# SiLU gates evicted by ACT alone, and the first attention queries prepared ahead of a branch

## The chip, the cores and the metric

The kernel runs on one core of a Trainium2 chip. The metric is the device time of one execution in microseconds (us). The engines are named as in the profile: PE (TensorE; its weight loads are PEld), DVE (VectorE), ACT (ScalarE), POOL (GpSimd) and SP (SyncE, which here only issues transfers). Each engine works through its own queue in order, and so does SP's queue of transfers.

## The reference, cut to what matters

One layer with 1024 prompt tokens and 64 sample tokens, width 1024, all in float32:

```
mod = silu(c) @ w_mod + b_mod                    # shift, scale, gate
h = rms_norm(x) * (1 + scale) + shift
z = h @ w_in     # q, k, v, indexer, zga, u, zgs, zma, zmb
o = sparse attention: 256 keys a query, chosen by a top-k of indexer scores
branch_a = (o * silu(zga)) @ w_attn_proj
y = state-space scan over u                      # complex diagonal, 64 states a group
branch_b = (glu(gelu(y)) * silu(zgs)) @ w_ssm_proj
x + gate * ((sigmoid(zma) * branch_a + sigmoid(zmb) * branch_b) @ w_out)
```

The change touches how `silu(zga)` and `silu(zgs)` are formed, when `gate` is computed, and when the first queries are rotated. What is computed stays the same.

## The kernel before

**Products as filler.** Every float32 product is made of three products of rounded halves (`mm3_parts`, L199): high by high, high by low (L202, L203) and low by high (L207). The projections of `h` that nothing waits for soon (q, u, zma, zmb, zga, zgs) are a list of 32 jobs of 128 columns, worked by one generator, `late` (L209, L634 to L645). A job has three chunks of 384, 384 and 320 tokens; a chunk is 24 matmuls in three **steps** of 8, and `next(late)` emits one step. The list has 288 steps. After a chunk its `evac` empties the PSUM tile `acc`, of which there are two (L100). The weights of the next job are loaded by SP into `raw` (L163, two buffers), rounded by ACT into `whi` (L157), and POOL makes the rest, `wlo` (L158). The jobs run in this order: q (4), u (4), 14 of zma and zmb, zga (4, `gate_a`), zgs (4, `gate_s`), and the last two of zma and zmb.

**The two gates.** `gate_a` (L616) and `gate_s` (L625) take the sigmoid of `acc` on ACT, then DVE multiplies it by `acc` (L621, L630); only then is `acc` free. `gate_a` goes on to POOL, which multiplies the attention output `oT` (L622); `gate_s` stores to DRAM.

**The stages after the keys.** First come the indexer scores, then the k and v projections. The top-k (L887) is a long run of DVE passes that ends in a branch on a value that DVE computes (`arms`, L967, with `select` inside). `N_TOPK` steps of filler are emitted ahead of the top-k beyond the q jobs, and `N_BR` steps after the branch: 6, and 6 + 9 + 4. Between those, `gates` (L1157) computes the gate row in two halves: a 2 MB load `gw`, 8 matmuls (L1172), a copy, a matmul by `sel` (L1177), a bias that DVE adds (L1180), a store. After the branch the pool `atq` is opened (L1204), in space that the top-k's tiles held. In it `att_queries` (L1002) loads a block of queries and its rotation table (L1006 to L1011), POOL rotates them (L1012 to L1014), and ACT and DVE split them (`stack_queries`, L254 to L260). `build_keys` (L986) transposes and splits the keys. Then `attention` runs, woven with filler.

**After attention** comes the state-space branch: `ssm_scan` (L1387), a serial chain on DVE, `ssm_fix` (L1406) for four groups q, and `ssm_out` (L1426), in which SP moves `zs` to `zq` (L1432) and PE multiplies (L1440, L1441). Filler is woven in at 3.2 steps a piece (L1469). Then the GELU (L1488: ACT, then two DVE passes that make `ghi` and `glo`), woven with filler at 3 steps, the rest of the filler (L1497), and the GLU products, which read `ghi` and `glo`. There POOL also makes `olo` (L1541), whose space is free when the last filler matmul has read `h`.

**What sets the order.** The program is traced in the order of the code, and a scheduler then fixes every engine's queue before the run: it goes by that order, but moves an instruction ahead where, by its own durations, an engine would be idle. So the queues hold an order that was planned with other durations than the chip's.

Of the kernel before, what the change touches and what calls it, by code (L numbers as in the profile page):

```python
# [33 lines left out]
P = 128  # L34
# [15 lines left out]
N_PRE = 6  # L50
N_TOPK = 6
N_BR = (6, 9, 4)
R_ATT = 1.15
# [30 lines left out]
def hybrid_step(ctx, tc, ins, outs):  # L84
# [27 lines left out]
    def bank1():  # L112
        return tpb().rearrange("p a b -> p (a b)")
# [23 lines left out]
    shcol = small.tile([P, KD, 2], F32, name="shcol")  # L137
    scs = small.tile([P, KD, 32], F32, name="scs")
    pool.memset(scs, 0.0)
    nhalf = small.tile([P, 1], F32, name="nhalf")  # L140
# [305 lines left out]
    c4 = small.tile([P, KD, 4], F32R, name="c4")  # L446
    dve.tensor_copy(c4[:, :, 0:2], scs[:, :, 0:2])
    c_rest = dve.tensor_tensor(c4[:, :, 2:4], scs[:, :, 0:2], c4[:, :, 0:2].bitcast(F32), op=OP.subtract)

# [17 lines left out]
    pool.memset(cz, 0.0)  # L467
    dve.tensor_copy(cz[:, :, 0:2], scs[:, :, 0:2])
    scr = rb.tile([P, 6, 512], F32, tag="t1", name="scr")
# [146 lines left out]
    def gate_a(m):  # L616

        def evac(c, t0, n, ps):
            s = tmp("sg")
            act.activation(s[:, :n], ps[:, :n], AF.Sigmoid)  # L620
            dve.tensor_tensor(s[:, :n], ps[:, :n], s[:, :n], op=OP.mult)  # L621
            pool.tensor_tensor(oT[:, m, t0:t0 + n], s[:, :n], oT[:, m, t0:t0 + n], op=OP.mult)  # L622
        return w_in, C_GA + m * P, evac

    def gate_s(m):  # L625

        def evac(c, t0, n, ps):
            s = tmp("sg")
            act.activation(s[:, :n], ps[:, :n], AF.Sigmoid)
            dve.tensor_tensor(s[:, :n], ps[:, :n], s[:, :n], op=OP.mult)  # L630
            sync.dma_start(gs_d[m, :, t0:t0 + n], s[:, :n])
        return w_in, C_GS + m * P, evac
# [36 lines left out]
    vnew = kvp.tile([64, 2, 64], F32, name="vnew")  # L669

    tk_ctx, ix_ctx = ExitStack(), ExitStack()
    tkp = tk_ctx.enter_context(tc.tile_pool(name="tkp", bufs=1, side="right"))
# [329 lines left out]
    def att_queries(b):  # L1002
# [10 lines left out]
        pool.tensor_tensor(qt[:, :, :nq], qt[:, :, :nq], cs, op=OP.mult)  # L1013
        pool.tensor_tensor(qt[:, :, :nq], qt[:, :, :nq], qw[:, :, :nq], op=OP.add)  # L1014
        st = atq.tile([P, 4, 2, P], F32R, tag="qs", name="qs")
        stack_queries(st, qt, 4, 4, nq)
        mx = small.tile([P, 4, 8], F32, tag="mx", name="mx", bufs=2)
        return st, mx

# [137 lines left out]
    def gates():  # L1157


        sel = small.tile([P, 2], F32, name="sel")  # L1160
        for b in range(2):
            dve.tensor_reduce(sel[:, b:b + 1], ident.rearrange("p (g r) -> p g r", r=32)[:, :, b],
                              axis=mybir.AxisListType.X, op=OP.add)
        for h in range(2):
            cols = slice(2 * D + h * 512, 2 * D + h * 512 + 512)
            ps = bank1()
            w = tokp.tile([P, KD, 512], F32, tag="wtok", name="gw")
            sync.dma_start(w, w_mod[:, cols].rearrange("(k p) c -> p k c", p=P))
            yield
            for k in range(KD):  # L1170
                g = 32 * (k % 4)
                pe.matmul(ps[g:g + 32], scs[:, k, :], w[:, k], start=(k < 4), stop=(k >= 4), skip_group_check=True)  # L1172
            yield
            r = wpool.tile([P, 528], F32, tag="raw", name="grow", bufs=RAW)[:, :512]
            act.copy(r, ps)
            o = bank1()[0:2]
            pe.matmul(o, sel, r, start=True, stop=True)  # L1177
            bm = wpool.tile([P, 528], F32, tag="raw", name="gbias", bufs=RAW)[0:2, :512]
            sync.dma_start(bm, ins["b_mod"][:, cols].to_broadcast([2, 512]))
            dve.tensor_tensor(bm, o, bm, op=OP.add)  # L1180
            sync.dma_start(gate_d[:, h * 512:h * 512 + 512], bm)
            yield

# [7 lines left out]
    kvs = kv()  # L1191
    run(kvs)
    while done[0] < n_q:
        next(late)
    q_stored = stored[0]
    for _ in range(N_TOPK):
        next(late)
    tk = topk(ixp)
    gate_steps = gates()
    next(gate_steps)  # L1200
    run(tk)
    ix_ctx.close()
    tk_ctx.close()
    atq = at_ctx.enter_context(tc.tile_pool(name="atq", bufs=2, side="right"))  # L1204
    for n, half in zip(N_BR, (3, 2, 0)):
        for _ in range(n):
            next(late)
        for _ in range(half):
            next(gate_steps, None)

    qw = wpool.tile([P, 4, P], F32, tag="ub", name="qw", bufs=1)
    pool.memset(qw, 0.0)
    kst = rb.tile([P, 2, 2, 1024], F32R, tag="t2", name="kst")
    build_keys(kst, None, [(ktok[:, t], P) for t in range(8)])
    with tc.issue_after(q_stored.ins):
        ready = att_queries(BO[0])

# [4 lines left out]
    def heads():  # L1222
# [4 lines left out]
        for i, b in enumerate(BO):  # L1227
# [6 lines left out]
            for h in range(8):  # L1234
                other = Head(b, h, st, mx, keys, vals, pt, other)
                yield other
                if h == QH and b < 8:
                    ready = att_queries(BO[i + 1])
                if h == VH and b == 8:
# [454 lines left out]
```

## Time and profile before

| | us |
|---|---|
| median of 3 runs | 1081.34 (1080.79 to 1082.34) |
| the profiled execution | 1083.0 |
| its span | 1081.2 |
| PE, PEld, DVE, ACT, POOL busy in the span | 987.0, 891.0, 673.0, 457.5, 290.6 |
| mean granted TensorE clock | 0.958 of full speed |

The span goes from the first to the last instruction; 1.8 us of the profiled execution lie outside of it. A busy engine is one with an instruction in it; for PE this includes time at half clock, so a stretch in which PE is busy throughout can still lose time. Where PE is idle, the view of waits names the engine and line whose end came last ahead of the waiting instruction.

### The profile page before, as it was taken

To read this page: it belongs to the slowest core of one execution; us is meant where nothing else is said; L and a number is where in the kernel's file an instruction comes from. 1 tells how busy PE (TensorE), PEld (TensorE's weight loads), DVE (VectorE), ACT (ScalarE), POOL (GpSimd) and SP (SyncE) were. 2 spreads that over 40 slices of the span, in tenths; PEclk is the share of its full clock that TensorE was granted. 3 is DMA by queue.
4 is the path that set the end of the run, shared out by engine and by line. 5 is a ranking of instruction groups with operands and counts; after the bars stand their busy time and mean duration, and the time that the engine had idled before them with its cause. 6 is when DMAs were issued, how large, how long until landed. Compare 5 with 4: busy or idle time off the path is not lost.

```text
span 1081.2 us, 16676 instructions
## 1 busy us (share of the span) xinstructions
PE 987.0 (91%) x5948; PEld 891.0 (82%) x5948; DVE 673.0 (62%) x1426; ACT 457.5 (42%) x973; POOL 290.6 (27%) x433
## 2 busy tenths in 40 slices
PE   7777999998799999999999991799997999999997
PEld 1466887998579999999898991799996999998786
DVE  6764888899247778877647799610107566654243
ACT  3575667221147666666533220122244344442122
POOL 3474202622330211222116260564114000001200
PEclk9797999998899999999999996899998999999999
DMA  8731201142451211112147331144764245534133
GB/s 294 220 92 30 77 2 47 52 160 63 133 125 26 62 54 51 56 59 80 57 99 125 97 97 25 43 96 97 166 188 118 88 148 168 160 105 156 53 128 112
DMA packets 141766, 108.41 MB, mean 100 GB/s; under 512 B 32894, under 2 KB 128680, under 8 KB 141680
## 3 DMA queue, kind: packets, MB, share of 16 engines
q1 hardware_dynamic: 140160, 105.05, 34.6%
q10 hardware_dynamic: 1232, 2.23, 0.6%
q8 instruction: 47, 0.77, 0.3%
q14 instruction: 39, 0.32, 0.1%
q0 software_dynamic: 288, 0.05, 0.0%
HBM read 77.79 MB, written 25.17 MB: 95 GB/s over the span
## 4 chain that ended last, share of the span: by engine, by line
PE 62%; DVE 22%; ACT 4%; issue 4%; POOL 3%; DMA 2%; SPq 2%; DVEq 0%; POOLq 0%; ACTq 0%
PE acc L202 12%; PE acc L207 12%; PE acc L203 11%; PE o L1084 4%; PE big L207 3%; PE big L203 3%; PE big L202 3%; PE tp L1067 3%; PE sc L1041 3%; DVE gt L910 2%; DVE near_v L917 2%; DVE sc L708 1%; PE big L695 1%; DVE t L1379 1%; DVE below L919 1%
## 5 line engine op out<-in xcount | busy, mean ns | idle before, releaser
L202 PE MATMUL acc<-hhi,whi 128*128 128x384 f32 (+1 forms) x768 | 258.8, 341 | 41.7 <-DVE sg L621 29.4
L203 PE MATMUL acc<-hlo,whi 128*128 128x384 f32 (+1 forms) x768 | 252.6, 333 | 0.0
L202 PEld LDWEIGHTS acc<-hhi,whi 128*128 128x128 f32 x768 | 147.0, 191 | 49.8 <-DVE sg L621 30.1
L207 PE MATMUL acc<-hhi,wlo 128*128 128x384 f32 (+1 forms) x768 | 148.2, 332 | 0.9 <-POOL wlo L158 0.9
L203 PEld LDWEIGHTS acc<-hlo,whi 128*128 128x128 f32 x768 | 147.1, 192 | 0.5
L158 POOL TENSOR_TENSOR wlo<-raw,whi 128x512 fp32r<-128x512 f32 x64 | 87.9, 1389 | 193.9 <-ACT whi L157 104.9
L207 PEld LDWEIGHTS acc<-hhi,wlo 128*128 128x128 f32 x768 | 128.5, 188 | 2.2 <-POOL wlo L158 1.5
L157 ACT CAST whi<-raw 128x512 fp32r<-128x512 f32 x64 | 38.2, 619 | 87.1 <-PE acc L203 49.3
L1071 ACT CAST pt<-tp 128x512 fp32r<-128x512 f32 (+3 forms) x112 | 49.4, 453 | 41.7 <-PE tp L1067 40.5
L1072 DVE TENSOR_TENSOR pt<-tp,pt 128x512 fp32r<-128x512 f32 (+3 forms) x112 | 57.1, 519 | 14.0 <-ACT pt L1071 12.7
L1051 ACT ACTIVATE pm<-pm,mx 128x1024 f32<-128x1024 f32 (+8 forms) x72 | 56.2, 780 | 20.0 <-DVE mx L1044 19.7
L1629 POOL TENSOR_TENSOR yh<-yh,gfin 128x512 f32<-128x512 f32 (+1 forms) x9 | 11.6, 1293 | 183.2 <-ACT xr L1625 183.2
L612 ACT COPY st<-acc 128x384 f32<-128x384 f32 (+1 forms) x60 | 27.7, 462 | 77.0 <-PE acc L207 72.7
L1044 DVE CUSTOM_DVE_ANT_0 pm<-sc,bias 128x512 f32<-128x512 f32 (+4 forms) x72 | 42.7, 594 | 26.0 <-PE sc L1041 24.9
L203 PE MATMUL acc<-wolo,mhi 128*128 128x512 f32 (+2 forms) x152 | 58.0, 386 | 0.0
L202 PE MATMUL acc<-wohi,mhi 128*128 128x512 f32 (+2 forms) x152 | 57.4, 381 | 0.0
L1041 PE MATMUL sc<-kst,qs 128*128 128x512 f32 (+3 forms) x192 | 52.1, 351 | 2.0 <-DVE mx L1044 1.3
L1067 PE MATMUL tp<-ident,pm 128*128 128x128 f32 (+2 forms) x328 | 53.0, 269 | 0.8 <-DVE pt L1072 0.6
L1084 PE MATMUL o<-pt,vst 128*128 128x256 f32 x288 | 47.6, 291 | 1.4 <-DVE pt L1072 1.2
L1067 PEld LDWEIGHTS tp<-ident,pm 128*128 128x128 f32 (+2 forms) x328 | 38.9, 139 | 9.5 <-DVE pt L1072 2.1
L708 DVE SCALAR_TENSOR_TENSOR sc<-relu,wi,sc 128x512 f32<-128x512 f32 (+5 forms) x42 | 42.7, 1019 | 3.8 <-ACT relu L706 1.0
L1013 POOL TENSOR_TENSOR qt<-qt,tab 128x512 f32<-128x512 f32 (+1 forms) x9 | 11.0, 1226 | 124.1 <-DMA qt<-q_d 117.2
(484 smaller groups left out, 2252.1 us busy)
## 6 DMA issues: line engine op xcount, KB each, us to landing
raw<-in_w_in SPq DMA_DIRECT2D x68, 256.0 KB
wm<-in_w_mod SPq DMA_DIRECT2D x16, 512.0 KB
xt<-in_x_prompt SPq DMA_DIRECT2D x8, 512.0 KB
gw<-in_w_mod SPq DMA_DIRECT2D x2, 2048.0 KB
raw<-in_w_out SPq DMA_DIRECT2D x16, 256.0 KB
xr<-in_x_prompt SPq DMA_DIRECT2D x16, 256.0 KB
ma_d<-st SPq DMA_DIRECT2D x16, 192.0 KB
mb_d<-st SPq DMA_DIRECT2D x16, 192.0 KB
```

The costliest lines, as they stand in the source:

```text
L158: rest_on[0].tensor_tensor(lo, raw, hi.bitcast(F32), op=OP.subtract)
L202: pe.matmul(ps, lhi(k), rhi(k), start=(k == 0), stop=False)
L203: pe.matmul(ps, lhi(k), rlo(k), start=False, stop=False)
L207: last_mm[0] = pe.matmul(ps, llo(k), rhi(k), start=False, stop=(k == nk - 1))
L708: dve.scalar_tensor_tensor(scores[b][:nq], r[:nq, :n], w, scores[b][:nq], op0=OP.mult, op1=OP.add, accum_out=sums[:nq, 0, col] if h == 4 e ...
L1041: pe.matmul(ps, self.st[:, self.h // 2, self.h % 2, :nq], self.keys[:, self.h // 4, j, c:c + m], start=(j == 0), stop=(j == 1))
L1044: dve.tensor_tensor_reduce(out=self.pm[:, c:c + m], in0=ps, in1=bias[self.b][:nq, c:c + m], op0=OP.add, op1=OP.min, scale=-0.125, scalar=t ...
L1051: act.activation(self.pm, self.pm, AF.Exp, bias=self.ng, scale=-1.0, accum_out=self.sm)
L1067: pe.transpose(tp[:rows, i, :nq], self.pm[:, c0:c0 + rows], ident[:nq, :nq])
L1071: act.copy(d0, tp[:rows, i0:i1, :nq])
L1072: dve.tensor_tensor(d1, tp[:rows, i0:i1, :nq], d0.bitcast(F32), op=OP.subtract)
L1084: last_mm[0] = pe.matmul(o, v[:rows, kt, pr // 2].rearrange("p a d -> p (a d)"), pk[:rows, j, i, :, :nq], start=(kt == 0 and j == 0), stop ...
```

## The change

1. `gate_a` and `gate_s`: one SiLU on ACT from `acc` into `s`, in place of a sigmoid on ACT and a product on DVE.
2. `atq` is opened ahead of the top-k's pools, in space of its own, and `att_queries` yields between the rotation and the split: loads and rotation of the first block are emitted once the q jobs are stored, ahead of the top-k; the split stays after the branch.
3. `gates`: its first load is emitted right after the k and v projections; both halves move one stage up, so that the first half is done and the second one loaded ahead of the top-k. The weights' operand `scs`, padded to 32 columns, is no longer kept in a tile of its own but copied by POOL beside each half of `gw`; the bias is added by POOL, after a copy by ACT.
4. Filler: 5 steps ahead of the top-k where there were 6, and 7 + 3 + 2 after the branch where there were 6 + 9 + 4: 8 steps fewer ahead of attention. The later ratios stay.

```diff
-N_TOPK = 6
-N_BR = (6, 9, 4)
+N_TOPK = (2, 3)
+N_BR = (7, 3, 2)
...
-    scs = small.tile([P, KD, 32], F32, name="scs")
-    pool.memset(scs, 0.0)
+    scs = small.tile([P, KD, 2], F32, name="scs")
...
         def evac(c, t0, n, ps):
             s = tmp("sg")
-            act.activation(s[:, :n], ps[:, :n], AF.Sigmoid)
-            dve.tensor_tensor(s[:, :n], ps[:, :n], s[:, :n], op=OP.mult)
+            act.activation(s[:, :n], ps[:, :n], AF.Silu)
             pool.tensor_tensor(oT[:, m, t0:t0 + n], s[:, :n], oT[:, m, t0:t0 + n], op=OP.mult)
...
             s = tmp("sg")
-            act.activation(s[:, :n], ps[:, :n], AF.Sigmoid)
-            dve.tensor_tensor(s[:, :n], ps[:, :n], s[:, :n], op=OP.mult)
+            act.activation(s[:, :n], ps[:, :n], AF.Silu)
             sync.dma_start(gs_d[m, :, t0:t0 + n], s[:, :n])
...
+    atq = at_ctx.enter_context(tc.tile_pool(name="atq", bufs=2, side="right"))
     tk_ctx, ix_ctx = ExitStack(), ExitStack()
...
         pool.tensor_tensor(qt[:, :, :nq], qt[:, :, :nq], qw[:, :, :nq], op=OP.add)
+        yield
         st = atq.tile([P, 4, 2, P], F32R, tag="qs", name="qs")
         stack_queries(st, qt, 4, 4, nq)
         mx = small.tile([P, 4, 8], F32, tag="mx", name="mx", bufs=2)
-        return st, mx
+        yield st, mx
...
         for h in range(2):
             cols = slice(2 * D + h * 512, 2 * D + h * 512 + 512)
+            w = tokp.tile([P, KD, 544], F32, tag="wtok", name="gw")
+            pool.memset(w[:, :, 512:], 0.0)
+            pool.tensor_copy(w[:, :, 512:514], scs)
+            sync.dma_start(w[:, :, 0:512], w_mod[:, cols].rearrange("(k p) c -> p k c", p=P))
+            yield
             ps = bank1()
-            w = tokp.tile([P, KD, 512], F32, tag="wtok", name="gw")
-            sync.dma_start(w, w_mod[:, cols].rearrange("(k p) c -> p k c", p=P))
-            yield
             for k in range(KD):
                 g = 32 * (k % 4)
-                pe.matmul(ps[g:g + 32], scs[:, k, :], w[:, k], start=(k < 4), stop=(k >= 4), skip_group_check=True)
-            yield
+                pe.matmul(ps[g:g + 32], w[:, k, 512:], w[:, k, 0:512], start=(k < 4), stop=(k >= 4), skip_group_check=True)
             r = wpool.tile([P, 528], F32, tag="raw", name="grow", bufs=RAW)[:, :512]
             act.copy(r, ps)
+            yield
             o = bank1()[0:2]
             pe.matmul(o, sel, r, start=True, stop=True)
+            act.copy(r[0:2], o)
             bm = wpool.tile([P, 528], F32, tag="raw", name="gbias", bufs=RAW)[0:2, :512]
             sync.dma_start(bm, ins["b_mod"][:, cols].to_broadcast([2, 512]))
-            dve.tensor_tensor(bm, o, bm, op=OP.add)
+            pool.tensor_tensor(bm, r[0:2], bm, op=OP.add)
             sync.dma_start(gate_d[:, h * 512:h * 512 + 512], bm)
-            yield
...
     run(kvs)
+    gate_steps = gates()
+    next(gate_steps)
     while done[0] < n_q:
         next(late)
     q_stored = stored[0]
-    for _ in range(N_TOPK):
-        next(late)
-    tk = topk(ixp)
-    gate_steps = gates()
-    next(gate_steps)
-    run(tk)
+
+    qw = wpool.tile([P, 4, P], F32, tag="ub", name="qw", bufs=1)
+    pool.memset(qw, 0.0)
+    with tc.issue_after(q_stored.ins):
+        first = att_queries(BO[0])
+        next(first)
+    for n in N_TOPK:
+        next(gate_steps)
+        for _ in range(n):
+            next(late)
+    run(topk(ixp))
     ix_ctx.close()
     tk_ctx.close()
-    atq = at_ctx.enter_context(tc.tile_pool(name="atq", bufs=2, side="right"))
-    for n, half in zip(N_BR, (3, 2, 0)):
+    for n in N_BR:
         for _ in range(n):
             next(late)
-        for _ in range(half):
-            next(gate_steps, None)
-
-    qw = wpool.tile([P, 4, P], F32, tag="ub", name="qw", bufs=1)
-    pool.memset(qw, 0.0)
+        next(gate_steps, None)
     kst = rb.tile([P, 2, 2, 1024], F32R, tag="t2", name="kst")
     build_keys(kst, None, [(ktok[:, t], P) for t in range(8)])
-    with tc.issue_after(q_stored.ins):
-        ready = att_queries(BO[0])
+    ready = next(first)
...
                 if h == QH and b < 8:
-                    ready = att_queries(BO[i + 1])
+                    ready = list(att_queries(BO[i + 1]))[1]
```

## Rows read from the trace of the kernel before

**Rows 1.** The page: busy us of each engine, share, instructions.
```profile
PE 987.0 (91%) x5948; PEld 891.0 (82%) x5948; DVE 673.0 (62%) x1426; ACT 457.5 (42%) x973; POOL 290.6 (27%) x433
```
**Rows 2.** Busy time by stretch: length, then each engine, granted clock, DMA share, GB/s.
```profile
250.00:300.00 50.00, 38.16 (x199) 33.06 (x198) 29.25 (x62) 8.82 (x19) 16.41 (x14) 0.83 0.41 113
...
650.00:700.00 50.00, 20.59 (x118) 19.74 (x118) 41.42 (x127) 5.22 (x11) 11.68 (x9) 0.73 0.13 33
...
800.00:850.00 50.00, 42.39 (x230) 40.65 (x229) 26.72 (x26) 20.90 (x30) 14.21 (x5) 0.90 0.47 139
...
286.00:291.00 5.00, 4.51 (x9) 2.31 (x10) 2.74 (x2) 2.02 (x6) 2.32 (x2) 0.50 0.47 89
...
681.00:686.00 5.00, 5.00 (x25) 5.00 (x26) 4.97 (x7) 0.62 (x1) 3.87 (x3) 0.71 0.12 29
...
830.00:835.00 5.00, 5.00 (x18) 5.00 (x19) 3.33 (x2) 0.00 (x0) 2.18 (x1) 0.59 0.21 63
```
**Rows 3.** Waits of PE, 640 to 700 us: total, times, longest.
```profile
PE acc L202 <- DVE sg L621: 29.4, 2, 28.4
```
**Rows 4.** Timeline from 215 to 290 us: start, length, engine, line, instruction, [idle before].
```profile
217.52 0.34 PE L202 MATMUL acc<-hhi,whi 128*128 128x384 f32 x1
...
221.74 0.34 PE L202 MATMUL acc<-hhi,whi 128*128 128x384 f32 x1
...
269.11 0.31 PE L202 MATMUL acc<-hhi,whi 128*128 128x320 f32 x1
...
276.47 0.26 DVE L790 TENSOR_SCALAR bias<-gts 128x384 bf16<-128x384 bf16 x1
...
280.46 1.26 POOL L1013 TENSOR_TENSOR qt<-qt,tab 128x512 f32<-128x512 f32 x1 [16.48 <-DMA qt<-q_d]
...
285.44 0.62 ACT L254 CAST qs<-qt 64x512 fp32r<-64x512 f32 x1 [12.60 <-POOL qt L1014]
...
286.49 0.69 PE L202 MATMUL acc<-hhi,whi 128*128 128x384 f32 x1 [7.61 <-ACT us L605]
...
287.21 1.65 DVE L260 TENSOR_TENSOR qs<-qt,qs 64x512 fp32r<-64x512 f32 x1
```
**Rows 5.** Timeline from 635 to 710 us, lines of DVE, ACT, SP and PE.
```profile
635.40 4.19 DVE L1382 TENSOR_TENSOR zs<-zs,t 128x272 f32<-128x272 f32 x1
...
652.54 0.49 ACT L620 ACTIVATE sg<-acc 128x384 f32<-128x384 f32 x1 [1.95 <-issue]
...
667.99 0.72 DVE L1421 TENSOR_TENSOR zs<-zs,f 128x544 f32<-128x544 f32 x1
...
670.22 1.92 SPq L1432 DMA_DIRECT2D zq<-zs  x3
...
684.20 0.37 SPq L164 DMA_DIRECT2D raw<-in_w_in  x1
...
687.50 0.62 ACT L157 CAST whi<-raw 128x512 fp32r<-128x512 f32 x1 [1.96 <-DMA raw<-in_w_in]
...
705.38 0.39 PE L1440 MATMUL tp<-uall,tq 128*128 128x136 f32 x2
```
**Rows 6.** Line 1421 on DVE: count, shortest/median/longest in ns, first and last start.
```profile
L1421 DVE TENSOR_TENSOR zs<-zs,f x8: 724/725/1700, 665.3 to 689.1; 128x544 f32<-128x544 f32 x8
```
**Rows 7.** Waits of PE, 800 to 850 us: total, times, longest.
```profile
PE big L203 <- DVE glo L1495: 4.0, 2, 3.1
PE big L202 <- DVE ghi L1494: 2.3, 1, 2.3
PE acc L202 <- ACT st L612: 1.3, 1, 1.3
```
**Rows 8.** Timeline from 810 to 835 us, lines of DVE and POOL.
```profile
813.76 1.29 DVE L1495 TENSOR_TENSOR glo<-gt,ghi 128x1088 fp32r<-128x1088 f32 x1
...
819.26 12.91 POOL L1541 TENSOR_TENSOR olo<-oT,ohi 128x1088 fp32r<-128x1088 f32 x4 [11.28 <-PE acc L207]
...
819.90 3.46 DVE L1495 TENSOR_TENSOR glo<-gt,ghi 128x1088 fp32r<-128x1088 f32 x1
```

More of the change, by code (lines that the diff above doesn't have):

```diff
@@ L446, in hybrid_step @@
     c4 = small.tile([P, KD, 4], F32R, name="c4")
-    dve.tensor_copy(c4[:, :, 0:2], scs[:, :, 0:2])
-    c_rest = dve.tensor_tensor(c4[:, :, 2:4], scs[:, :, 0:2], c4[:, :, 0:2].bitcast(F32), op=OP.subtract)
+    dve.tensor_copy(c4[:, :, 0:2], scs)
+    c_rest = dve.tensor_tensor(c4[:, :, 2:4], scs, c4[:, :, 0:2].bitcast(F32), op=OP.subtract)
     def chain(*gens):
@@ L467, in hybrid_step @@
     pool.memset(cz, 0.0)
-    dve.tensor_copy(cz[:, :, 0:2], scs[:, :, 0:2])
+    dve.tensor_copy(cz[:, :, 0:2], scs)
     scr = rb.tile([P, 6, 512], F32, tag="t1", name="scr")
```

## The prediction

> **What bounds the kernel now.** I read the page first: PE is busy for 987.0 of 1081.2 us and no other engine for more than 673.0 [rows 1]. So the time is PE's work plus the time in which PE stands still or runs at half clock. Next, busy time in stretches of 50 us. In most of them PE is busy almost throughout; after the start there are three large holes [rows 2]: 250 to 300 (38.16 us busy, clock 0.83), 650 to 700 (20.59, clock 0.73) and 800 to 850 (42.39, clock 0.90). Then the waits and the timeline there, to see what ends last. I call the holes A, B and C.
>
> *A.* PE waits 7.61 us for ACT to evict `acc` (L605). ACT was idle for 12.60 us: at the head of its queue stood the split of the first queries, which waited for POOL's rotation; POOL waited 16.48 us for the loads [rows 4]. The loads were issued right behind DVE's last work of the top-k, at 276.47 + 0.26 = 276.7, because the query tile lies in the top-k's space. The clock was granted at 0.50 for the next 5 us, in which PE was busy for 4.51 [rows 2]; at full rate that work takes half, so 2.3 us are lost. A is worth 7.6 + 2.3 = 9.9 us.
>
> *B.* PE waits 29.4 us in two pieces for DVE's product L621 [rows 3]. ACT's sigmoid of the second gate chunk had begun at 652.54 [rows 5], but DVE's queue holds the product behind most of the scan and of the fixes, so both `acc` tiles stay taken. After it, 5 us at clock 0.71 [rows 2] lose 5 x 0.29 = 1.5. B is worth 30.9 us.
>
> *C.* PE waits 4.0 + 2.3 + 1.3 = 7.6 us, mostly for DVE's two passes over the GELU [rows 7]. A pass that takes 1.29 us alone takes 3.46 beside POOL's `olo` [rows 8], which starts when the last filler matmul ends. Then 5 us at clock 0.59 [rows 2] lose 2.1. C is worth 9.7 us.
>
> **The change part by part.** The filler work itself is the same in total: 288 steps, wherever they stand. A 384-column chunk starts 221.74 - 217.52 = 4.22 us after the one before [rows 4]; the 320-column one, scaled by columns, takes 3.52; so a step takes (2 x 4.22 + 3.52) / 9 = 1.33 us, and the 8 moved steps are 10.6 us of cover that leave A's neighbourhood and come up behind the scan.
>
> *SiLU on ACT.* 24 products leave DVE. ACT's function has the tile's shape as before, and I take its 0.49 us [rows 5] unchanged; ACT is idle for most of B, so a longer one, even doubled, stays hidden behind a 4.22 us chunk. `acc` then depends on ACT alone and B's wait loses its cause. What is late next? PE runs on into the order planned for it and meets L1440, the first product that needs the scan's result, which stood at 705.38 [rows 5]; with 30.9 us taken out it stands at 674.5. Its input: the first fix ends at 667.99 + 0.72 = 668.7; SP issues three transfers from 670.22 to 672.1 [rows 5], a fourth some 0.6 later. The nearest landing is that of a weight load, issued at 684.20 and used from 687.50 [rows 5], 3.3 us; so the data is there at about 676. Also, POOL's multiplications of `oT` and its weight splits no longer stand still beside the fixes. L1421 takes 0.72 us alone and up to 1.70 beside POOL [rows 6], 1.0 us more. Some four POOL instructions (two multiplications, two splits) fall between 652 and 669, so DVE comes 4 us later, and the data at 680. That is a new wait of 5.5 us. Bounds: none, if POOL's work falls beside instructions with one SBUF input, and 14 us with four collisions of 3.5 us each, as L1382 had one (4.19 us, against 0.72 for L1421 of twice the columns) [rows 5]. I take 5.5, since L1421 is the instruction that is hit. B returns 25.4.
>
> The Trainium skill (SBUF — State Buffer, Who interferes with whom) says that a DVE instruction with two SBUF inputs and a GpSimd instruction that reads SBUF exclude each other for a whole instruction. That speaks against freeing POOL here. By it the four POOL instructions would cost their full lengths and the wait would be a microsecond or two longer than by L1421's row.
>
> *Queries ahead of the branch.* Six transfers on SP (table, queries, four shifted rows) and three POOL instructions of 1.26 us [rows 4] move ahead of the top-k's end. They depend only on the last q store. In SP's queue weight loads stand behind them, in POOL's queue weight splits. Rotated, they let ACT's split pass at once, and A loses its cause. Price: POOL's 3 x 1.26 = 3.8 us can stand ahead of a split that PE needs. Bounds 0 (POOL has long idle stretches beside the top-k) and 3.8; I take the middle, 1.9.
>
> *Less filler ahead of attention.* After the branch PE had begun its steps at 269.11 [rows 4]. Now 12 steps, 16.0 us, stand there, to about 285. The top-k ends at 276.7, and DVE's two query subtractions, at most 1.65 us each [rows 4], end at 280. The cover is thinner by 10.6 us but still reaches 5 us beyond; I cost it at nothing. If the cover were gone, it would cost up to those 10.6. A returns 9.9 - 1.9 = 8.0.
>
> *Gate row.* The matmuls, transfers and copies are the same in number; two small copies by ACT and a little POOL work (a pad, a bias of 2 x 512) are added, and DVE gives up two 2 x 512 additions. Beside engines that are idle in this stretch (ACT 8.82, POOL 16.41 of 50 us) [rows 2] I cost this at nothing; between a microsecond lost and one won.
>
> *The 8 steps behind the scan.* They come to stand ahead of the GLU, while ACT and DVE do the GELU: 10.6 us of PE work against a hole of 9.7, and `olo`, tied to the last filler matmul, starts later than DVE's passes. It will instead slow DVE at the start of the GLU: it lasts 12.91 us and made a pass longer by 3.46 - 1.29 = 2.2 us [rows 8]. I take one such delay of 2.2 as reaching PE; bounds 0 and the whole hole. C returns 7.5.
>
> Sum: 8.0 + 25.4 + 7.5 = 40.9 us from the profiled execution's 1083.0, which is 1042.1. That execution lies 1.7 us above the median of the runs, so for a median I say **1040.4**. If every hole closed: 50.5 us, 1030.8 as a median.
>
> **Rivals.** In each the time is put as a median, so 1081.3 less what returns.
>
> *The queue of SP takes B's place.* SP's transfers of `zs` stand in its queue ahead of weight loads, as at 670.22 and 684.20 [rows 5], and wait for the first fix. PE, no longer held, has 11 steps from 652.5 until the job whose weights may be behind them: 8 more than 3 of the old order, so 14.6 us, to 667. The loads would go out at 676.7, with the 4 us from above, and the weights be usable at 680.6. PE stands 13.6 us and loses 1.5 to the clock: B returns 15.8. For it: the order of the two kinds in the queue. Against: the loads ran one job ahead before B. 1050.
>
> *C stays.* If the planned order puts the 8 steps among the scan's pieces and not behind the last of them, the GELU is as bare as before. C returns nothing: 1048. Against it: the weaving ratios are unchanged, so what is not used earlier is left over at the end.
>
> *The rotation isn't early in effect:* its transfers are behind stores in SP's queue and the split still blocks ACT. A returns nothing: 1048.5.
>
> *POOL against DVE throughout, slower than before.* Place: the scan and the fixes, 12 multiplications and about as many weight splits of POOL beside serial DVE work. If each costs 3.5 us, as L1382's row, DVE's chain is 24 x 3.5 = 84 us longer and the scan's data comes at 676 + 84 = 760, 85.5 us after PE: 1081.3 - 50.5 + 85.5 = 1116. It decides from 2.0 us a collision ((50.5 - 1.5) / 24). Against it: 1.0 us at L1421 [rows 6], and many POOL instructions fall beside ACT or PSUM work of DVE or none.
>
> **How the numbers follow.** Forecast 0.62 (own range 1031 to 1046); SP's queue 0.15; C stays 0.09; rotation late 0.06; POOL against DVE 0.05; 0.03 for no difference through several of these together. The range 1029 to 1057 holds the forecast, the next three, and a mix of two of them. A measurement of this kernel tells about 0.2%, 2.2 us, from no change. All but the last two cases are faster: 0.92 faster, 0.03 the same, 0.05 slower.
>
> **What would show it.** Right: no wait of PE for DVE's `sg`, since no such instruction exists; PE busy for over 43 us of the 50 in which the scan ends; the query loads landed before the top-k's end and no ACT idle time of 12 us behind it; PE waits for `ghi` and `glo` under 3 us. Wrong: a wait of ten us or more of PE at L1440 or at a weight split L158 while DVE is in the fixes (B moved), at the first scores L1041 (cover gone), or at L203 behind `glo` (C stays); or DVE's L1379 to L1421 much longer in sum than before.

## The result, and the profile after

The changed kernel takes **1051.76 us** as a median (1050.64 to 1053.00) against 1081.63 for the kernel before, measured beside it: a ratio of 0.9724 (95% interval 0.9708 to 0.9741). That is faster by 2.8%, inside the range of the prediction, and 11.4 us above its time. The profiled execution took 1050.65 us with a span of 1048.8, so between the two profiled spans 32.4 us went; between the medians it is 29.9.

The page, one line, and busy time by stretch in the three places of [rows 2] (columns as there):

```profile
PE 978.5 (93%) x5948; PEld 887.9 (85%) x5948; DVE 661.5 (63%) x1400; ACT 459.0 (44%) x975; POOL 296.0 (28%) x438
```
```profile
250.00:300.00 50.00, 35.43 (x187) 29.36 (x186) 28.26 (x59) 9.89 (x19) 20.42 (x18) 0.80 0.39 108
...
650.00:700.00 50.00, 38.44 (x237) 37.22 (x237) 30.54 (x66) 7.87 (x16) 26.35 (x32) 0.86 0.40 95
...
800.00:850.00 50.00, 50.00 (x302) 50.00 (x301) 32.23 (x46) 18.56 (x38) 11.20 (x4) 1.00 0.33 99
```

Three holes, three answers. The last stretch is full at full clock: C is closed. The middle one is half filled: B came back in part. The first one is no better than it was (38.16 us busy at clock 0.83 before): A came back not at all. PE's waits from 240 to 1000 us (total, times, longest) name what stands there now:

```profile
PE acc L201 <- ACT whi L156: 14.6, 2, 9.5
PE acc L201 <- ACT sg L619: 11.6, 1, 11.6
...
PE tp L1330 <- POOL ca L1321: 1.8, 1, 1.8
```

No wait for DVE's gate product is left [rows 3], none for `ghi` or `glo` [rows 7]. In their place PE waits 14.6 us for weights in A, and 11.6 us for ACT's eviction in B.

**The sum by events.** Four events cut the time into parts that can be compared: the first transpose of the keys, the first product of the scan, the first product of the GLU and its third block. Of the kernel before (timeline; the product of the scan at 705.38 stands in [rows 5]):

```profile
310.75 0.49 PE L994 MATMUL tp<-ident,ktok 128*128 128x128 f32 x3
...
819.02 0.34 PE L202 MATMUL big<-ghi,whip 128*128 128x384 f32 x1
...
853.40 0.34 PE L202 MATMUL big<-ghi,whip 128*128 128x384 f32 x1
```

Of the kernel after:

```profile
300.26 0.93 PE L992 MATMUL tp<-ident,ktok 128*128 128x128 f32 x7
...
673.06 0.66 PE L1442 MATMUL tp<-uall,tq 128*128 128x136 f32 x2
...
799.70 0.34 PE L201 MATMUL big<-ghi,whip 128*128 128x384 f32 x1
...
823.64 0.34 PE L201 MATMUL big<-ghi,whip 128*128 128x384 f32 x1
```

The keys come 10.5 us earlier, but 8 filler steps (10.6 us) are no longer ahead of them: A returned 0. From there to the scan's first product the same filler is done (421 matmuls of each of its first two kinds in either kernel), and the lead grows from 10.5 to 32.3: B returned 21.8, of which 29.4 - 11.6 = 17.8 are the wait itself. Smaller waits in this stretch give 2.6 (PE is idle for 36.4 us of it before and 16.0 after), and the same work takes 1.5 us less (358.2 us busy, then 356.8). Up to the GLU the lead shrinks to 19.3: the 8 steps are made up for here, and 13.0 - 10.6 = 2.4 us are lost. They are lost to the clock, since PE's idle time between the two events is about the same (2.6 us before, 2.3 after): it is 0.61 from 673 to 676 us, behind the stall that is left in B, and 0.72 from 716 to 722, behind the wait of 1.8 us. By the GLU's third block the lead is 29.8: C returned 10.4. The last 2.6 us of the 32.4 arise evenly over the output stage, the last 105 us, which the change doesn't touch: there a group of 24 matmuls takes 5.44 us where it took 5.60, at a granted clock of 1.00 in both. Why is open; the medians, 29.9 apart, don't show it.

**A, why nothing came back.** The timeline of the changed kernel from 262 to 288 us:

```profile
263.20 2.10 POOL L1011 TENSOR_TENSOR qt<-qt,tab 128x512 f32<-128x512 f32 x1 [5.72 <-DMA qt<-q_d]
...
269.23 1.25 POOL L1182 TENSOR_TENSOR gbias<-grow,gbias 2x512 f32<-2x512 f32 x1
269.30 0.62 ACT L253 CAST qs<-qt 64x512 fp32r<-64x512 f32 x1 [1.31 <-POOL qt L1012]
...
270.83 0.41 SPq L163 DMA_DIRECT2D raw<-in_w_in  x1
...
274.38 0.69 PE L201 MATMUL acc<-hhi,whi 128*128 128x384 f32 x1 [5.05 <-ACT whi L156]
...
281.57 0.69 DVE L259 TENSOR_TENSOR qs<-qt,qs 64x512 fp32r<-64x512 f32 x1
282.29 0.38 SPq L1004 DMA_DIRECT2D qt<-q_d  x1
282.77 0.44 SPq L163 DMA_DIRECT2D raw<-in_w_in  x1
...
286.15 0.62 ACT L156 CAST whi<-raw 128x512 fp32r<-128x512 f32 x1 [11.83 <-DMA raw<-in_w_in]
...
286.82 0.69 PE L201 MATMUL acc<-hhi,whi 128*128 128x384 f32 x1 [9.52 <-ACT whi L156]
```

The rotation itself did what it should: ACT splits the queries at 269.30, ahead of the end of the top-k, and isn't blocked by them any more. Something else now ends last. The gate row's two tiles lie in the two `raw` buffers through which every weight passes. Its bias addition (L1182) stands in POOL's queue behind the three instructions of the rotation, the first of which waited for its transfer. Not before it is done can the next weight load go out, at 270.83, and PE waits 5.05 us. The second wait begins in SP's queue: the *second* query block's load (L1004, at 282.29) needs the one query tile, which DVE's split frees at 281.57 + 0.69, and the next weight load stands behind it.

**B, what took its place.** From 649 to 674 us:

```profile
649.05 0.50 ACT L619 ACTIVATE sg<-acc 128x384 f32<-128x384 f32 x1 [2.45 <-issue]
...
660.90 0.07 DVE L1426 MEMSET zs<- 128x8 f32 x1
...
661.03 1.26 SPq L1434 DMA_DIRECT2D zq<-zs  x2
...
665.02 0.99 SPq L163 DMA_DIRECT2D raw<-in_w_in  x2
...
668.64 1.30 ACT L156 CAST whi<-raw 128x512 fp32r<-128x512 f32 x2 [19.10 <-DMA raw<-in_w_in]
...
669.85 0.43 ACT L619 ACTIVATE sg<-acc 128x320 f32<-128x320 f32 x1
...
670.33 0.69 PE L201 MATMUL acc<-hhi,whi 128*128 128x384 f32 x1 [11.56 <-ACT sg L619]
```

Read it from the last line up. PE waits for the third chunk's eviction. That chunk's products end at 652.5, but two casts of weights stand ahead of the eviction in ACT's queue and have waited 19.10 us for their load. The load stands in SP's queue behind the transfers of the scan's result, and these wait for the first fix, whose last write to `zs` (L1426) ends at 660.97. This is the rival of SP's queue, reached one step earlier than it was drawn: not PE's next weights, but the eviction behind their casts holds PE. The SiLU takes the 0.49 to 0.50 us of the sigmoid.

**C.** DVE's four passes L1497, of which one took 3.46 us beside `olo` before [rows 8], all take 1.29, because `olo` starts at 799.94 with the GLU (line 1497: shortest/median/longest in ns, first and last start):

```profile
L1497 DVE TENSOR_TENSOR glo<-gt,ghi x4: 1292/1293/1294, 781.8 to 791.5; 128x1088 fp32r<-128x1088 f32 x4
```

### The profile page after: what moved, and what is told of

Same layout as the page of the kernel before. It is cut to its first block, busy times and chain, and to the rows that moved or that the text cites. A ratio compares the mean times of both kernels' runs of the same rounds, so it can differ in the third digit from the quotient of the medians.

```text
span 1048.8 us, 16634 instructions
## 1 busy us (share of the span) xinstructions
PE 978.5 (93%) x5948; PEld 887.9 (85%) x5948; DVE 661.5 (63%) x1400; ACT 459.0 (44%) x975; POOL 296.0 (28%) x438
## 4 chain that ended last, share of the span: by engine, by line
PE 61%; DVE 20%; ACT 5%; POOL 4%; issue 4%; DMA 3%; SPq 1%; POOLq 0%; DVEq 0%; ACTq 0%
PE acc L201 12%; PE acc L206 12%; PE acc L202 12%; PE o L1083 3%; PE big L201 3%; PE big L202 3%; PE big L206 3%; PE sc L1040 3%; PE tp L1066 3%; DVE gt L908 2%; DMA raw<-in_w_in 2%; DVE sc L706 2%; DVE near_v L915 1%; DVE t L1381 1%; POOL hlo L559 1%
## 5 line engine op out<-in xcount | busy, mean ns | idle before, releaser
L201 PE MATMUL acc<-hhi,whi 128*128 128x384 f32 (+1 forms) x768 | 257.2, 339 | 26.2 <-ACT whi L156 14.6
L1496 DVE CAST ghi<-gt 128x1088 fp32r<-128x1088 f32 x4 | 3.2, 808 | 103.1 <-DMA raw<-in_w_in 100.0
L1631 POOL TENSOR_TENSOR yh<-yh,gfin 128x512 f32<-128x512 f32 (+1 forms) x9 | 11.6, 1292 | 173.3 <-ACT xr L1627 173.3
```

The costliest lines, as they stand in the source:

```text
L201: pe.matmul(ps, lhi(k), rhi(k), start=(k == 0), stop=False)
```

## The experiments

All times are medians, each ratio taken against the kernel before as it ran beside it. The median of before lay between 1081.6 and 1083.4 from one group of runs to the next, so a difference between runs of two groups is good to a microsecond or two. The first four runs take the change apart.

**SiLU alone**, in the kernel before (one of the two gates is shown, the other is edited alike):

```diff
-            act.activation(s[:, :n], ps[:, :n], AF.Sigmoid)
-            dve.tensor_tensor(s[:, :n], ps[:, :n], s[:, :n], op=OP.mult)
+            act.activation(s[:, :n], ps[:, :n], AF.Silu)
```

> The kernel before, with SiLU on ACT in both gates and nothing else. Theory 1 (the wait for DVE's product is the one cause of the hole at 650 to 700 us, and what is left of it in the changed kernel, 11.6 us, is SP's queue): no wait of PE for DVE's sg, a new wait of 5 to 18 us in its place, the holes at 280 us (7.6 us) and at 820 us (7.6 us) as before; 1059 to 1070 us. Rival (the hole is DVE's serial chain whatever frees the PSUM tiles): PE stands about as long at the first product after the scan; 1078 us or more. Rival (the product was worth the whole hole): no wait above 3 us there; 1051 us.

1075.31 us, ratio 0.9929 (0.9906 to 0.9952). PE's longest wait:

```profile
PE acc L202 <- ACT sg L620: 20.4, 1, 20.4
```

The wait of 29.4 us for DVE becomes one of 20.4 for ACT, with SP's weight load behind the transfers of the scan as in the changed kernel. The cause is the one expected; the size is above all that was named, and the time outside what was expected.

**The product back on DVE**, in the changed kernel (the same lines in reverse):

> The changed kernel with the sigmoid on ACT and the product on DVE back in both gates, all else as changed. The gate chunks come 8 steps (10.6 us of PE work) later in the queue than in the kernel before, nearer to the end of the scan. Theory 1: PE waits for DVE's sg about 28.4 - 10.6 = 18 us where it now waits 11.6 for ACT: 1056 to 1062 us. Rival (SiLU alone carries the gain, the place of the steps nothing at this hole): a wait of 28 us again, 1068 us or more.

1066.70 us, ratio 0.9843 (0.9825 to 0.9861). PE waits 26.1 us for `sg` from DVE and 14.9 for weights in A. This is nearer the rival: the moved steps hardly shorten the wait for DVE. It also shows that A's wait for weights has nothing to do with SiLU.

**The moved steps back**, in the changed kernel:

```diff
-N_TOPK = (2, 3)
-N_BR = (7, 3, 2)
+N_TOPK = (2, 4)
+N_BR = (7, 8, 4)
```

> The changed kernel with 6 steps ahead of the top-k and 19 behind the branch, as before. Theory 1 (the 8 steps close the hole ahead of the GLU and were not missed ahead of attention): PE waits for ghi, glo and the eviction 6 to 8 us in all around 790 to 820 us, the waits for weights after the branch stay at about 14 us: 1060 to 1066 us. Rival (the steps only shift where PE waits): the waits after the branch fall by what comes up ahead of the GLU; within 3 us of the changed kernel's 1051.8.

1071.45 us, ratio 0.9897 (0.9859 to 0.9935), five microseconds above what was expected:

```profile
PE acc L201 <- ACT sg L619: 20.6, 1, 20.6
PE acc L201 <- ACT whi L156: 14.8, 2, 9.7
PE big L202 <- DVE glo L1497: 4.0, 2, 3.1
...
PE big L201 <- DVE ghi L1496: 2.3, 1, 2.3
```

Two readings. C's waits are back to the tenth [rows 7], so C belongs to the moved steps alone. And A's wait for weights is the same (14.8 against 14.6) with 8 steps more ahead of the keys, so it is not a lack of cover. What was not expected is B: 20.6 us in place of 11.6. SiLU without the moved steps leaves 20.4 us there (the first run) to 20.6, the moved steps without SiLU 26.1 (the run above) to 26.3 (the next one), both together 11.6. The traces show what the steps do for B:

```profile
673.31 0.07 DVE L1426 MEMSET zs<- 128x8 f32 x1
...
680.33 0.69 PE L201 MATMUL acc<-hhi,whi 128*128 128x384 f32 x1 [20.57 <-ACT sg L619]
```

PE stops at the same place of the filler as in the changed kernel (544 matmuls of each kind since 200 us in either) and at nearly the same time, 659.8 here and 658.8 there. But with 8 more steps ahead of the keys the scan comes later, and its first fix, on which the transfers and behind them the weight loads wait, ends at 673.38 in place of 660.97. So the steps that are moved away from the keys shorten B too, because they bring the scan forward.

**The moved steps alone**, in the kernel before:

```diff
-N_TOPK = 6
-N_BR = (6, 9, 4)
+N_TOPK = 5
+N_BR = (7, 3, 2)
```

> The kernel before with 5 steps ahead of the top-k and 7, 3, 2 after the branch, and nothing else. Theory 1: the hole ahead of the GLU closes (about 10 us and more), the wait for DVE's sg shrinks by about 10 us since the gates come 10.6 us of work later, and the hole behind the branch grows by up to 10 us, since the first scores wait for the queries as long as before: 1061 to 1072 us. Rival (steps only shift where PE waits): 1079 us or more.

1067.58 us, ratio 0.9857 (0.9839 to 0.9875): C is closed, PE waits 26.3 us for DVE in B and 8.5 for the eviction `us` in A. Against the 1083.2 us of the kernel before beside them the steps alone return 15.6 us, SiLU alone 7.9, and all of the change but SiLU 16.5. So the early queries and the gate row add 0.9 to the steps, about nothing.

**A: the gate row in tiles of its own.** One tile for each half of the row, from the pool `atq` and in the buffers of the queries' split tile, holds what lay in the two `raw` buffers:

```diff
-            r = wpool.tile([P, 528], F32, tag="raw", name="grow", bufs=RAW)[:, :512]
+            rb2 = atq.tile([P, 1024], F32, tag="qs", name="grow"); r = rb2[:, :512]
...
-            bm = wpool.tile([P, 528], F32, tag="raw", name="gbias", bufs=RAW)[0:2, :512]
+            bm = rb2[0:2, 512:1024]
```

> The changed kernel with the two tiles of the gate row in the space of the second query block's split tile, so that the two `raw` buffers serve weights alone. Theory (in hole A, PE waits for weights because the gate row holds both `raw` buffers while its bias addition stands in POOL's queue behind the rotation of the first queries): the weight loads go out before 262, PE's first wait for `whi` (5.05 us) goes, and since the order of SP also changes behind it (weights ahead of the second block's query load) the second (9.5 us) shrinks to under 4; hole A then returns 8 to 13 us, the keys' transposes start at about 288 in place of 300.3, and the time is 1038 to 1045. Rival (the 8 steps taken away from here are the cover that is missing, and weights are late only because nothing else is): PE gets its weights and then stands as long for the queries' or keys' copies on ACT; the sum of its waits between 260 and 305 stays at 12 to 15 us and the time at 1050 to 1054.

1040.12 us (1039.59 to 1041.93), ratio 0.9602 (0.9575 to 0.9628). Busy time by stretch and PE's waits from 240 to 1000 us:

```profile
250.00:300.00 50.00, 43.68 (x242) 35.33 (x242) 40.43 (x74) 18.48 (x34) 22.82 (x20) 0.97 0.54 137
```
```profile
PE acc L201 <- ACT sg L619: 11.1, 1, 11.1
PE tp L1178 <- ACT grow L1175: 4.7, 1, 4.7
```

Both waits for weights are gone, a smaller one for the gate row itself is left, and the stretch holds 43.68 us of PE work at clock 0.97 in place of 35.43 at 0.80. The keys' transposes start at 287.95, 12.3 us earlier. The theory holds and the rival falls: the cover was enough, its weights came late. In this run three weight loads, from 275.82 to 281.40, also go out ahead of the second query block's load, at 285.76, so both causes named above go at once and are not told apart. This is the best version of all, 11.6 us below the change for two lines. B is as it was, at 11.1.

**A: the early queries undone**, in the changed kernel. The loads and the rotation go back behind the branch, their tiles into the space that the top-k frees:

```diff
-    atq = at_ctx.enter_context(tc.tile_pool(name="atq", bufs=2, side="right"))
...
-    with tc.issue_after(q_stored.ins):
-        first = att_queries(BO[0])
-        next(first)
...
+    atq = at_ctx.enter_context(tc.tile_pool(name="atq", bufs=2, side="right"))
...
+    with tc.issue_after(q_stored.ins):
+        first = att_queries(BO[0])
+        next(first)
     ready = next(first)
```

> The changed kernel with one part undone: the first queries are loaded and rotated behind the branch as before, their tiles in the space that the top-k frees; SiLU, the moved steps and the new order of the gate row stay. Theory (the early queries do what they should, but what they return is eaten by weights that come late): ACT's queue is held again for about 12 us behind the top-k, with 8 steps less as cover, so the sum of PE's waits between 260 and 305 is 20 to 26 us in place of 14.6, and the time 1057 to 1064. Rival (the early queries give nothing, or cost, because the rotation on POOL is what holds the gate row's bias and with it the weights): the sum of the waits stays at 15 us or below and the time at 1047 to 1053.

1052.73 us, ratio 0.9711 (0.9686 to 0.9736): not to be told from the changed kernel. But neither story is right, since the wait is a third one (PE's waits, then SP's timeline):

```profile
PE tp L1172 <- DMA gw<-in_w_mod: 15.2, 1, 15.2
```
```profile
275.71 0.33 SPq L1005 DMA_DIRECT2D tab<-in_rope_feat  x1
276.14 0.39 SPq L1167 DMA_DIRECT2D gw<-in_w_mod  x1
```

The table of the rotation, whose tile lies in the top-k's space again, waits at the head of SP's queue for the top-k to end, and the load of the gate row's weights stands behind it. So this run doesn't measure what the early queries are worth by themselves; it shows only that undoing them costs nothing within the change.

**B: the scan's transfers by another queue.** `sync.dma_start(zq...)` becomes `pool.dma_start(zq...)`, nothing else:

> The changed kernel with the transfers of `zs` into `zq` issued by POOL's queue instead of SP's; nothing else. Theory (the wait of 11.6 us in hole B is SP's queue: the weight loads stand behind the `zq` transfers, which wait for the first fix): the four loads go out by about 656, ACT's casts no longer hold the evictions, the wait of PE for `sg` falls below 3 us. Part of it comes back as a wait for `wlo` (its subtractions now stand in POOL's queue behind `zq`) or for the first product of the scan, together 2 to 6 us. Time 1043 to 1049. Rival 1 (the scan's data is what is really late): the wait moves whole to L1442 and the time stays within 1050 to 1053. Rival 2 (POOL's weight splits now fall beside the fixes of DVE, L1423 goes from 0.72 to 1.7 us): the fixes take 5 us or more longer, the first product waits over 8 us, and the time is above 1050.

1074.00 us, ratio 0.9905 (0.9868 to 0.9941), 22 us *slower* than the changed kernel:

```profile
PE acc L206 <- POOL wlo L157: 15.1, 1, 15.1
```
```profile
657.26 1.97 POOL L1434 DMA_DIRECT2D zq<-zs  x3 [21.11 <-DVE zs L1426]
659.23 2.52 POOL L157 TENSOR_TENSOR wlo<-raw,whi 128x512 fp32r<-128x512 f32 x2
```

The same mistake one queue further: POOL now stands 21.11 us with the transfers at the head of its queue, and the subtractions that make `wlo` stand behind them, without which neither PE goes on nor the `raw` buffers come free. The theory put POOL's price at 2 to 6 us, far too low. Whether it is right about SP this run can't tell: the first weight loads go out at 660.55, no earlier than these subtractions let them, and not by 656 as expected.

**Both edits together:**

> Both edits together (gate row in tiles of its own, `zq` transfers by POOL's queue). If the two waits are independent, the gains add: 1051.8 - (8 to 13) - (3 to 9) = 1031 to 1041, and the time is below the forecast of 1040.4 for the change itself. If the holes only pass work on to one another (filler that is not used in A comes up in B), it is within 2 us of the better of the two single edits.

1060.56 us, ratio 0.9782 (0.9755 to 0.9808). Neither of the two expected times, since one of the edits loses; but they add: the gate row's tiles return 1074.0 - 1060.6 = 13.4 us here, 11.6 without the other edit.

**B: loads first, in a pair of runs.** The first run adds one turn of the filler (3 steps) ahead of the first transfers of the scan's result (the edit yields before `ssm_out` issues them, so the turn stands ahead of the transfers, not behind them as its expectation has it):

```diff
-            yield from ssm_out(q)
+            yield from chain(iter([0] * (q == 0)), ssm_out(q))
```

> The changed kernel with one more turn of the filler (3 steps) between the transfers of the first part of the scan's result and the products that read them; the place of those transfers in SP's queue, ahead of the weight loads, stays. It is the counterpart of the run in which the loads go first. Theory (PE stands in hole B because the weight loads are behind transfers that wait for the first fix): the wait of PE stays at 10 to 13 us and the time at 1049 to 1054. Rival (what PE lacks is filler ahead of the first product of the scan): the wait falls by the 3 steps, 4 us, and the time to 1046 to 1049.

The second adds to that a tie by which these transfers are issued behind the last weight load:

```diff
-        sync.dma_start(raw, src)
+        last_raw[0] = sync.dma_start(raw, src)
...
-                sync.dma_start(zq[64 * j:64 * j + 64, :, g2, :], z4[64 * g2:64 * g2 + 64, j, rs, 0:NCH])
+                with tc.issue_after(last_raw[0].ins): sync.dma_start(zq[64 * j:64 * j + 64, :, g2, :], z4[64 * g2:64 * g2 + 64, j, rs, 0:NCH])
```

> As the run with one more turn of the filler, and in addition each transfer of `zs` is issued behind the weight load that is last at that point, so that in SP's queue two weight loads stand ahead of the first one; queue and engines stay. Theory: those loads go out some 20 us earlier, ACT's casts no longer hold the evictions, PE's wait for `sg` in hole B falls from 11.6 to under 3 us; some 1 to 4 us come back as a wait for the scan's data at L1442 or for the next weights. Time 1040 to 1046. Rival (as with POOL's queue, the in-order wait only moves to another instruction): PE stands 8 us or more at one place between 650 and 700 and the time is 1048 or above.

The turn alone: 1063.62 us, ratio 0.9823 (0.9803 to 0.9844), and PE still waits 11.3 us for `sg`: three steps of filler do nothing for B. With loads first: 1057.06 us, ratio 0.9756 (0.9733 to 0.9780). SP's timeline and PE's waits from 640 to 690 us in that run:

```profile
644.62 1.64 SPq L163 DMA_DIRECT2D raw<-in_w_in  x2
...
667.30 2.60 SPq L1434 DMA_DIRECT2D zq<-zs  x4
```
```profile
PE tp L1443 <- DMA zq<-zs: 3.2, 1, 3.2
```

The wait of 11.3 us becomes one of 3.2 for the scan's own data. In hole B the theory holds: the order in SP's queue is its cause. The time falls by 6.6 us within the pair. Both times expected were missed, since the extra turn costs some 11 to 12 us elsewhere. Behind 690 us PE waits 10.6 us with loads first, 11.8 with the turn alone, 2.3 in the changed kernel; with loads first:

```profile
PE tp L1330 <- POOL ca L1321: 3.4, 1, 3.4
PE acc L201 <- ACT whi L156: 3.2, 1, 3.2
PE tp L1443 <- DMA zq<-zs: 2.3, 2, 2.1
...
```

The turn alone has the same waits, each within 1.1 us.

**Loads first, with the gate row's tiles:**

> The loads-first edit together with the gate row in tiles of its own. The two holes are 370 us apart and share no wait: if the gains add, the time is 1040.1 less what the loads-first edit gives alone, so 1029 to 1035, the lowest of all; PE's waits between 240 and 850 sum to under 20 us. Rival (filler that is used in one hole is missing in the next): C opens again by 3 us or more (waits for `ghi`, `glo` or `st` from 790 on) and the time is within 3 us of 1040.

1044.97 us, ratio 0.9653 (0.9632 to 0.9673): B's wait is 3.2 us, yet the time is 4.9 above the gate row's tiles alone. No wait for `ghi` or `glo` comes back, but behind 690 us PE waits 11.4 us in place of 2.4. Against loads first alone the gate row's tiles return 12.1 us, so that gain does add.

**The same, with a turn of filler taken out behind the first products** (and only the transfers of the first part tied):

```diff
-            yield
+            if q: yield
```

> Gate row in tiles of its own and weight loads first in SP's queue, as in the run of both, but the turn of filler that was added ahead of the first products of the scan is taken back behind them, so that the filler left for the end is what the change leaves, and only the first transfer is tied to a weight load. Theory (the run of both lost behind 690 what it won at 655 because three filler steps were spent early): PE's waits from 690 to 860, 11.4 us in that run against 2.4 with the gate row's tiles alone, fall to 5 or less, and the time is 1033 to 1039, the lowest of all. Rival (the scan's later parts are late because PE now reaches them sooner than POOL's tables, SP's transfers and the weights behind them): the waits from 690 on stay at 8 us or above and the time at 1040 to 1046.

1046.62 us (1042.84 to 1049.73), ratio 0.9643 (0.9600 to 0.9686). The waits behind 690 us are still 11.9 us, so how much filler is left for the end is not what costs. That is what the rival said (its time is missed by 0.6 us), but its reason, that PE now reaches the scan's later parts sooner, isn't shown: the turn alone has these waits too, with B's 11.3 us still standing. What all four runs have in common is the turn ahead of the first transfers. Loads first without that turn was not run, so what the order of SP's queue returns by itself is open beyond the 6.6 us within the pair.

## Why the prediction was right or wrong

**Right: what bounds, and the sign.** The time is PE's work, its waits and its clock; in every experiment it moved with waits of PE in the three holes or in the stage behind B. The range held the result because it was drawn to hold three rivals too; the forecast's own range, 1031 to 1046, did not. That 1051.76 is close to the 1050 of the rival of SP's queue is luck: it had A return 8.0 and B 15.8, where they returned 0 and 21.8. Of the signs of being right, the early query loads, no wait for DVE's `sg` and none for `ghi` and `glo` came about; PE's busy time in B is 38.44 us and not over 43, and ACT again stands idle for 11.83 us behind the top-k, now for a weight load.

**A, forecast 8.0, returned 0.** The step that failed is the price of the edits, not the gain: ACT was freed as forecast. "Queries ahead of the branch" put the price at 0 to 3.8 us of POOL's own time ahead of a split, and "Gate row" at nothing beside idle engines. The price was in buffers and queues: the gate row keeps both `raw` buffers while it waits in POOL's queue behind the rotation, and the second block's query load waits in SP's queue for the one query tile ahead of a weight load. The rows that could have told it were named in the text (six transfers in SP's queue, weight loads behind them), but only the *moved* transfers were followed, not the block that comes next. With the gate row in tiles of its own A's 11.6 us come back at once. The cover, costed at nothing, was rightly costed: the wait for weights is 14.6 us with and 14.8 without the moved steps.

**B, forecast 25.4, returned 21.8.** The wait that remains was put at 5.5 us, at the first product of the scan; it is 11.56 us, at an eviction. This is the rival "the queue of SP takes B's place", with the chance 0.15 and a wait of 13.6. What was argued against it, that the loads ran one job ahead before B, is true of the job that was loaded at 635 and not of the next. The prediction had nothing in B for the moved steps, which bring the scan forward (see the run with the steps back).

Three readings in that sum were off. The fourth transfer of the scan's result was put 0.6 us behind the other three; in the kernel before it went out at 684.62, behind a weight load. The first product that reads this result is L1441, 0.2 us behind L1440, which multiplies the scan's input. And 0 and 14 us bound the delay, not the wait: with the data at 676 and PE at 674.5 they make it 1.5 to 15.5. The estimate of the collisions held where it could be tested: with the weight loads first, five instructions of DVE between 652 and 664 us are 4.8 us longer in sum beside POOL, where the forecast had 4, and PE waits 3.2 us for the scan's data, though with one more turn of filler ahead of it. In the changed kernel POOL is idle from 650.6 to 669.3, so these collisions don't take place.

The Trainium skill (SBUF — State Buffer, Who interferes with whom) says that a DVE instruction with two SBUF inputs and a GpSimd instruction that reads SBUF exclude each other for a whole instruction. One row bears on it: in the run with POOL's queue an instruction of line L1421, whose inputs `car` and `arf` lie in SBUF as those of POOL's subtractions do, took 3.43 us, 2.71 more than the usual 0.72, while POOL worked for 2.52 us on two of them. That agrees with the page.

```profile
658.90 3.43 DVE L1421 TENSOR_TENSOR f<-car,arf 128x544 f32<-128x544 f32 x1
```

In the changed kernel four collisions between 640 and 651 us lengthen the scan by 3.9 us in sum, ahead of the first fix on which SP's transfers wait; those from 669 us on are behind it.

**C, forecast 7.5, returned 10.4.** The mechanism was right, both sizes off. The 2.2 us that `olo` was to cost at the start of the GLU reach nobody: PE has no wait there. And the loss to the clock was read from one slice of 5 us at 0.59 (2.1 us); the slice ahead of it had the clock at 0.50 as well, with 2.74 us of PE work, another 1.4 us:

```profile
825.00:830.00 5.00, 2.74 (x8) 2.23 (x8) 4.97 (x3) 0.00 (x0) 5.00 (x3) 0.50 0.02 5
```

**Between B and C, 2.4 us lost**, for which the sum had no term: the clock is low behind the stall that is left in B and behind a wait for POOL's tables. In sum 0 + 21.8 - 2.4 + 10.4 = 29.8, the 29.9 us of the medians, where 40.9 were forecast.

**Interactions.** SiLU returns 7.9 us alone and 14.9 on top of the rest; the steps 15.6 alone and 19.7 on top. The terms were summed as if independent; they meet in B, where either alone leaves a wait of over 20 us: SiLU makes PE depend on the first fix, by way of the weight loads, and the moved steps bring that fix forward by 12.4 us.

## What to carry to other kernels

When an edit moves a transfer or a small tile, list what stands behind it in each in-order queue and which shared buffers it holds until *its* last reader has run; here a bias addition of 2 x 512 elements and a load for the next block cost as much as the wait that the edit took away. A transfer that waits for late data should not stand ahead of weight loads, and putting it on another engine's queue here only moved the standstill to what that engine had to do next. And when an edit needs a second one to make room for it, run that second one alone: the added turn of filler by itself cost 11.9 us, more than the order of the loads won.

## What was not expected

That a queue other than SP's made it 22 us worse: POOL stood 21.11 us at the head of its queue, though POOL is busy for only 28% of the changed kernel's span. And that three filler steps, 4 us of work that was only brought forward, cost 1063.62 - 1051.76 = 11.9 us through waits in the 130 us behind them.
